# A hybrid attention block on one core: the keys' rotary step joins the plan, shuffles are given longer landing times, and filler products are placed otherwise

## The chip, the cores and the metric

The kernel runs on one core of one Trainium2 chip. The core has five engines that matter here, each with its own instruction queue that is worked off in order: TensorE (PE, matrix products and transposes), VectorE (DVE), ScalarE (ACT), GpSimd (POOL) and SyncE (SP), which here only starts DMA transfers. The metric is device time in microseconds of one execution; lower is better. The times before are the median of three runs.

## The reference

One encoder block, all in float32, for 512 real tokens of width 1024, ahead of which stand 16 learned meta tokens (528 columns in the kernel):

```python
u = rms_norm(h, pre_mix_gain[l])
proj = u @ w_in[l]
qa, ka, va, qb, kb, vb, g = jnp.split(proj, SPLITS, axis=-1)
qa = rope(qa...); ka = rope(ka...); qb = rope(qb...); kb = rope(kb...)
o_swa = windowed_gqa_sink_attention(qa, ka, va, attn_sink[l], pos, is_real)
o_diff = differential_attention(qb, kb, vb, lam, lambda_init, diff_subln_gain[l], is_key)
gates = jax.nn.sigmoid(g + b_gate[l]); g_swa, g_diff = gates[..., :D_MODEL], gates[..., D_MODEL:]
merged = g_swa * (o_swa @ w_branch_swa[l]) + g_diff * (o_diff @ w_branch_diff[l])
h = h + rms_norm(merged @ w_out[l], post_mix_gain[l])
u = rms_norm(h, pre_ffn_gain[l]); gate_up = u @ w_ffn_in[l]
f = (jax.nn.silu(gate_up[..., :D_FF]) * gate_up[..., D_FF:]) @ w_ffn_out[l]
h = h + rms_norm(f, post_ffn_gain[l])
```

The first branch (o_swa) is windowed attention with 16 query heads in four groups, each group with one key head, a band of three blocks of 128 keys, the meta keys and a sink. The second branch (o_diff) has 8 heads; each subtracts two softmaxes over all keys and is normalized over its own 128 channels. `rope` rotates the two halves of a head's 64 channels by angles that depend on the position.

## The kernel before

Every float32 matrix is split into a high part that TensorE takes exactly (`float32r`) and a low remainder; a product is then three matmuls (`mm3`, L283: high x high, high x low, low x high). A weight tile of 128 output channels is loaded by SyncE (512 KB), its high part is cast by ScalarE, and the remainder is subtracted by GpSimd or VectorE. There are three buffers each for the raw weights (`wr`), the high parts (`wh`) and the low parts (`wl`). A product of such a tile over 512 columns is 24 matmuls.

The work runs in these stages:

1. Start (to L505). The inputs are loaded and split, keys (`kA`, `kB`) and half of the values of the first branch are projected, and the factors of the first normalization are worked out. The rotation tables `rot` are multiplied by them. Then the keys' rotary step: `rope` (L466) takes the raw keys `kraw` in two halves of 264 columns, multiplies them by the tables on VectorE (L470, L471), adds on GpSimd (L472), and `split` writes high and low parts into a tile `hl`. Twelve DMA shuffles bring this to a layout that the score products can take, `KK[g]` for four groups: two from `hl` into the upper partitions of `KK[g]` (L488) and one that doubles these into the lower 64 partitions (L489). After these come loads of the lambda vectors and of two masks.
2. The plan (L508 to L979). `Plan` is a small planner that runs when the program is built. Every step is a `task` with an engine, a cost in us, the buffers that it reads, writes or keeps, and a priority. `Plan.run` walks through time: for each engine it takes the task that can start first, on TensorE by its priority alone, on the others by its ready time plus a slack from its priority. A task that writes a buffer follows all earlier writers and users of that buffer. Buffers stand in slots (`hl` 1, `kk` 4, `q` 8, `wr`, `wh`, `wl` 3, `ta` 2, `tb` 1, `S` 1). The result is the order of instructions on each engine; what really happens at run time is set by semaphores, and each engine follows its order. The planner's times are never used on the chip.
   In the plan are: the values of the first branch (`v_swa`), queries of four groups (`q_swa`, L650), the gates of the first branch (`gate`), the 16 units of windowed attention (`s_swa` scores and softmax, `t_swa` transposes and products with V), the heads of the second branch (`qk`, `vd`, `s_diff`, `t_diff`), the output projection of the first branch (`b1`, eight products) and the gates of the second (`gate2`, eight products). `rope_t` (L546) is the planned form of `rope`; `move` (L568) is the planned DMA shuffle, with 0.6 us of SyncE's time and a landing time `land` after it.
   On TensorE, attention steps have priorities 0, 1 and 8; the projections have 20 and a running number of the weight tile, and fill what the attention leaves ("fillers").
   The keys are not in the plan: the four `KK` tiles are given to it as held buffers that are ready at 9.0 us (L628 to L632). The tile `hl` is a single buffer, which the keys and each later group or head use in turn.
3. After the plan: the output projection of the second branch (L990), the sum, `w_out`, the second normalization, and the feed-forward layer (to L1175). Order and code of it are untouched.

At the start of the plan the engines' queues are joined with those of the start stage: within each of both the order is the program's, and the two are interleaved by the framework's scheduler.

Of the kernel before, what the change touches and what calls it, by code (L numbers as in the profile page):

```python
# [20 lines left out]
P = 128  # L21
# [215 lines left out]
def encoder(ctx, tc, I, out, dbg=None):  # L237
# [227 lines left out]

    def rope(hl, psa, psb, c0, n, o0, scale=None):  # L466

        ta = atp.tile([P, 2, HALF], F32, tag="ta", name="ta", bufs=2)[:, :, 0:n]
        tb = atp.tile([P, 2, HALF], F32, tag="tb", name="tb")[:, :, 0:n]
        dve.tensor_tensor(out=ta, in0=psa.unsqueeze(1).broadcast_to([P, 2, n]), in1=rot[:, 1:3, c0:c0 + n], op=ALU.mult)  # L470
        dve.tensor_tensor(out=tb, in0=psb.unsqueeze(1).broadcast_to([P, 2, n]), in1=rot[:, 0:2, c0:c0 + n], op=ALU.mult)  # L471
        pool.tensor_tensor(out=ta, in0=ta, in1=tb, op=ALU.add)  # L472
        split(hl[:, :, 0, o0:o0 + n], hl[:, :, 1, o0:o0 + n], ta, scale=scale)
        return ta

    def hl_tile():
        return zp.tile([P, 2, 2, KX], F32R, tag="hl", name="hl")

    hl = hl_tile()
    KK = [zp.tile([P, 2, KX], F32R, tag="kk", name="KK", bufs=4) for _ in range(4)]  # L480
    for s in range(2):
        cs = slice(s * HALF, (s + 1) * HALF)
        ta = rope(hl, kraw[0][:, cs], kraw[1][:, cs], s * HALF, HALF, s * HALF)
        if s == 0:
            split(hl[:, :, 0, EXT:KX], hl[:, :, 1, EXT:KX], ta[:, :, 0:NMETA])
    for g in range(4):
        for i in range(2):
            sp.dma_start(out=KK[g][32 * i:32 * i + 32].bitcast(F32), in_=hl[32 * g:32 * g + 32, i].bitcast(F32))  # L488
        sp.dma_start(out=KK[g][64:128].bitcast(F32), in_=KK[g][0:64].bitcast(F32))  # L489
# [56 lines left out]
    def rope_t(hl, pa, pb, c0, n, p0, o0, scale):  # L546
# [5 lines left out]
        def half(t, src, i):  # L552
# [3 lines left out]
        oh_, ol_ = (lambda: hl.t[:, :, 0, o0:o0 + n]), (lambda: hl.t[:, :, 1, o0:o0 + n])  # L556
# [5 lines left out]
        T("ACT", 0.18 + 0.55 * m, lambda: act.activation(out=oh_(), in_=ta.t[:, :, 0:n], func=AF.Copy, scale=scale),  # L562
          r=[ta], w=[hl], prio=3)
        T("DVE", 0.19 + 0.58 * m,
          lambda: dve.scalar_tensor_tensor(out=ol_(), in0=ta.t[:, :, 0:n], scalar=scale, in1=oh_().bitcast(F32),
                                           op0=ALU.mult, op1=ALU.subtract), r=[ta], w=[hl], prio=3, port=True)

    def move(out, in_, r, w, dep=(), land=1.6):  # L568
        return T("SP", 0.6, lambda: sp.dma_start(out=out().bitcast(F32), in_=in_().bitcast(F32)), r=r, w=w, dep=dep,  # L569
                 prio=2, land=land)  # L570
# [57 lines left out]
    KB = [pl.held("kk", KK[g]) for g in range(4)]  # L628
    MK = [pl.held("rt", t) for t in (mk1, mk2)]
    PV = [pl.held("tr", t) for t in pV]  # L630
    for b in KB:
        pl.ready(b, 9.0)  # L632
    for b in MK:
        pl.ready(b, 5.0)

# [30 lines left out]
    def s_swa(u):  # L666
# [11 lines left out]
        for hh in range(4):  # L678
# [3 lines left out]
            def prod(hh=hh, S=S):  # L682
                for x in range(2):
                    pe.matmul(out=Sw2[:, S.slot, 0:nk], lhsT=QS[g][hh].t[:, i * P:(i + 1) * P],  # L684
                              rhs=KK[g][:, x, r0:r1], start=(x == 0), stop=(x == 1))
            Ssteps[u].append(T("PE", 2 * mm_t(nk), prod, r=[QS[g][hh], KB[g]], w=[S], keep=[S0], prio=1))
# [16 lines left out]
    def t_swa(u):  # L703
# [5 lines left out]
        for n, (o, kb) in enumerate(blocks):  # L709
# [6 lines left out]
            Ttr[u].append(T("PE", 0.436, trans, r=ph, w=[tr], keep=[pt], prio=0, chain="tr"))  # L716
# [41 lines left out]
    def qk(h):  # L758
# [11 lines left out]
        for c in range(2):  # L770
            K = sb("kk", [P, 2, EXT], F32R, "Kd", 4, zp)
            Q = sb("q", [P, EXT], F32R, "Qd", 8)
            for i in range(2):
                move(lambda i=i, K=K: K.t[32 * i:32 * i + 32], lambda i=i, c=c: hl.t[64 + 32 * c:96 + 32 * c, i, :, 0:EXT],
                     [hl], [K], land=1.9)
            move(lambda K=K: K.t[64:128], lambda K=K: K.t[0:64], [], [K], land=2.2)
            for i in range(2):
                for x in range(2):
                    b = 2 * x + i
                    move(lambda b=b, Q=Q: Q.t[32 * b:32 * b + 32, 0:NTOK],  # L780
# [479 lines left out]
```

## Time and profile before

| what | value |
|---|---|
| median of 3 runs (lowest, highest) | 1012.42 us (1012.09, 1013.39) |
| profiled execution, its own time | 1011.81 us |
| its span, first to last instruction | 1010.0 us |
| mean granted TensorE clock | 0.988 of full speed |
| TensorE busy | 968.4 us, 96% |
| VectorE, ScalarE, GpSimd busy | 565.2, 450.6, 281.4 us |
| DMA moved | 109.33 MB |

The profile is of one execution. Its span is from the first to the last instruction, and the execution took 1.8 us more than that. An engine's "idle before" a row is the time in which it had nothing to run before that instruction, and the arrow names what it waited for last. The stages by time: start to about 25 us, first branch about 25 to 225, second branch about 225 to 551, the rest to the end.

### The profile page before, as it was taken

The numbers are of one execution on the slowest core, as the hardware profiler recorded it, in microseconds if no ns is written. First come the engines' busy times: TensorE is split into PE (matmuls) and PEld (weight loads), VectorE is DVE, ScalarE is ACT, GpSimd is POOL, SyncE is SP. The second block draws the span as 40 slices with busy tenths as digits, with TensorE's granted clock in tenths as the row PEclk, the third lists the DMA queues.
The fourth block names the chain that finished last, engine by engine and source line by source line (L and its number), as shares of the span: only waits on it lengthen the run. The fifth ranks groups of instructions, "written<-read, shape, count | busy, mean of one in ns | idle before, by whom it ended". The sixth has DMA issues, their size and how long they took to land.

```text
span 1010.0 us, 14259 instructions
## 1 busy us (share of the span) xinstructions
PE 968.4 (96%) x5355; PEld 833.9 (83%) x5355; DVE 565.2 (56%) x1015; ACT 450.6 (45%) x828; POOL 281.4 (28%) x242
## 2 busy tenths in 40 slices
PE   9879998999899999999799999999999999999997
PEld 9767888889698989998688888998888888888885
DVE  5736885888585647778664774853333333323224
ACT  6316773776455536366655343443223223222121
POOL 1343444533142232342221421464343310000000
PEclk9999999999999999999899999999999999999999
DMA  9463123241424342432623461252323333324222
GB/s 342 119 167 107 43 66 84 71 138 43 127 63 127 91 119 58 112 106 55 180 64 128 143 231 41 84 193 99 105 86 102 104 90 98 105 85 145 61 64 83
DMA packets 37140, 109.33 MB, mean 108 GB/s; under 512 B 6080, under 2 KB 6592, under 8 KB 37072
## 3 DMA queue, kind: packets, MB, share of 16 engines
q1 hardware_dynamic: 37072, 108.42, 35.4%
q8 instruction: 42, 0.69, 0.3%
q14 instruction: 26, 0.21, 0.1%
HBM read 87.04 MB, written 2.10 MB: 88 GB/s over the span
## 4 chain that ended last, share of the span: by engine, by line
PE 64%; DVE 3%; SPq 2%; DMA 1%; issue 1%; ACT 0%; DVEq 0%; ACTq 0%
PE pr L288 14%; PE pr L287 14%; PE pr L286 14%; PE Sd L818 3%; PE wk L288 2%; PE wk L287 2%; PE wk L286 2%; SPq L569 2%; PE tr L858 1%; PE acc L288 1%; PE tr L288 1%; PE acc L287 1%; PE tr L287 1%; PE acc L286 1%; PE tr L286 1%; PE Od L871 1%
## 5 line engine op out<-in xcount | busy, mean ns | idle before, releaser
L252 POOL TENSOR_TENSOR wl<-wr,wh 128x768 fp32r<-128x768 f32 (+1 forms) x76 | 168.0, 2212 | 244.7 <-ACT wh L271 159.4
L286 PE MATMUL pr<-xh,wh 128*128 128x264 f32 (+1 forms) x616 | 200.3, 325 | 0.0
L288 PE MATMUL pr<-xh,wl 128*128 128x264 f32 (+1 forms) x616 | 196.7, 319 | 2.2 <-DVE wl L252 2.2
L287 PE MATMUL pr<-xl,wh 128*128 128x264 f32 (+1 forms) x616 | 197.1, 320 | 0.2 <-DVE xl L378 0.2
L271 ACT CAST wh<-wr 128x1024 fp32r<-128x1024 f32 x78 | 82.1, 1052 | 232.1 <-PE pr L287 95.7
L252 DVE TENSOR_TENSOR wl<-wr,wh 128x1024 fp32r<-128x1024 f32 (+2 forms) x110 | 111.0, 1010 | 118.2 <-ACT wh L271 110.1
L288 PEld LDWEIGHTS pr<-xh,wl 128*128 128x128 f32 x616 | 116.4, 189 | 10.9 <-DVE wl L252 2.4
L287 PEld LDWEIGHTS pr<-xl,wh 128*128 128x128 f32 x616 | 116.7, 189 | 7.6 <-DVE xl L378 0.4
L286 PEld LDWEIGHTS pr<-xh,wh 128*128 128x128 f32 x616 | 116.7, 189 | 7.1
L287 PE MATMUL pr<-ul,wh 128*128 128x512 f32 (+1 forms) x304 | 110.7, 364 | 0.3 <-DVE ul L252 0.3
L286 PE MATMUL pr<-uh,wh 128*128 128x512 f32 (+1 forms) x304 | 110.9, 365 | 0.0
L288 PE MATMUL pr<-uh,wl 128*128 128x512 f32 (+1 forms) x304 | 110.6, 364 | 0.0
L528 ACT CAST wh<-wr 128x1024 fp32r<-128x1024 f32 x56 | 58.3, 1046 | 29.8 <-PE pr L287 19.6
L287 PEld LDWEIGHTS pr<-ul,wh 128*128 128x128 f32 x304 | 57.3, 189 | 9.6 <-DVE ul L252 0.5
L286 PEld LDWEIGHTS pr<-uh,wh 128*128 128x128 f32 x304 | 57.4, 189 | 9.2
L288 PEld LDWEIGHTS pr<-uh,wl 128*128 128x128 f32 x304 | 57.3, 189 | 9.0
L823 DVE TENSOR_REDUCE nm<-Sd 128x1 f32<-128x528 f32 x64 | 45.1, 705 | 34.0 <-PE Sd L818 33.3
L559 POOL TENSOR_TENSOR ta<-ta,tb 128x528 f32<-128x528 f32 (+1 forms) x24 | 34.7, 1446 | 76.2 <-DVE tb L553 56.2
L818 PE MATMUL Sd<-Kd,Qd 128*128 128x264 f32 x256 | 44.2, 295 | 11.0 <-DMA wr<-in_w_in_dram 5.3
L698 POOL TENSOR_SCALAR p<-p,rc 128x272 f32<-128x272 f32 (+1 forms) x64 | 37.6, 603 | 61.5 <-DVE rc L696 61.5
L308 POOL TENSOR_TENSOR r3y<-r3v,mhalf 128x1 f32<-128x1 f32 x4 | 2.2, 550 | 186.7 <-DVE r3v L307 186.7
L687 DVE CUSTOM_DVE_ANT_0 p<-Sw,mk,nsink 128x272 f32<-128x272 f32 (+1 forms) x64 | 34.6, 565 | 27.8 <-PE Sw L684 26.4
(369 smaller groups left out, 1993.8 us busy)
## 6 DMA issues: line engine op xcount, KB each, us to landing
wr<-in_w_in_dram SPq DMA_DIRECT2D x50, 512.0 KB, 3.7
wr<-in_w_fi_dram SPq DMA_DIRECT2D x50, 512.0 KB, 3.5
wr<-in_w_fo_dram SPq DMA_DIRECT2D x22, 512.0 KB, 3.5
Kd<-hl SPq DMA_DIRECT2D x32, 132.0 KB, 2.4
Kd<-Kd SPq DMA_DIRECT2D x16, 264.0 KB, 3.3
Q<-hl SPq DMA_DIRECT2D x64, 64.0 KB, 2.0
Qd<-hl SPq DMA_DIRECT2D x64, 64.0 KB, 2.5
wr<-in_w_bs_dram SPq DMA_DIRECT2D x8, 512.0 KB, 3.6
```

Of the source, the lines that this page charges most:

```text
L252: (eng or dve).tensor_tensor(out=lo, in0=src, in1=hi.bitcast(F32), op=ALU.subtract)
L271: act.copy(out=wh, in_=raw)
L286: pe.matmul(out=ps, lhsT=ah, rhs=bh, start=first, stop=False)
L287: pe.matmul(out=ps, lhsT=ah, rhs=bl, start=False, stop=False)
L288: pe.matmul(out=ps, lhsT=al, rhs=bh, start=False, stop=last)
L528: T("ACT", 1.05, lambda: act.copy(out=wh.t, in_=wr.t), r=[wr], w=[wh], prio=pr_)
L559: T("POOL", 0.05 + 1.3 * m, lambda: pool.tensor_tensor(out=ta.t[:, :, 0:n], in0=ta.t[:, :, 0:n], in1=tb.t[:, :, 0:n], op=ALU.add), r=[tb], ...
L569: return T("SP", 0.6, lambda: sp.dma_start(out=out().bitcast(F32), in_=in_().bitcast(F32)), r=r, w=w, dep=dep, prio=2, land=land)
L687: T("DVE", 0.21 + 0.5 * c, lambda hh=hh, S=S, h=h: dve.tensor_tensor_reduce(out=pt.t[:, hh, 0:nk], in0=Sw2[:, S.slot, 0:nk], in1=mask, sca ...
L698: T("POOL", 0.2 + 0.43 * c, lambda z=z: pool.tensor_scalar(out=pt.t[:, z, 0:nk], in0=pt.t[:, z, 0:nk], scalar1=rc.t[:, z:z + 1], scalar2=1 ...
L818: pe.matmul(out=S.t[:, s, 0:HALF], lhsT=Q[c].t[:, i * P:(i + 1) * P], rhs=K[c].t[:, x, s * HALF:(s + 1) * HALF], start=(x == 0), stop=(x = ...
L823: T("DVE", 0.71, lambda S=S, c=c, one=one: dve.tensor_reduce(out=nm.t[:, c, one], in_=S.t[:, :, 0:HALF], axis=AX.XY, op=ALU.min), r=[S], w ...
```

## The change

- The keys' rotary step and its 12 shuffles leave the start stage and become tasks of the plan. `rope` and `hl_tile` are gone; `rope_t` takes the raw keys and, by `more`, also writes the 16 meta columns a second time behind the others. The `hl` tile and the four `KK` tiles are now the plan's buffers. The loads of lambda and masks keep their place in the start stage, which now has no shuffles ahead of them.
- Landing times in the plan: shuffles 2.7 us instead of 1.6 (queries) and 1.9 (second branch's keys), the doubling of key tiles 4.0 instead of 2.2.
- Planned TensorE costs: score products get 0.08 us more in the first branch and 0.12 in the second; a group of four transposes 0.5 us instead of 0.436.
- Fillers: of the eight `b1` products, three, three and two stand with heads 0, 1 and 2, instead of two, three and three. `gate2` takes separate conditions for its weight loads (`early`) and its products (`dep`): tiles 4 to 7 now come first, their loads from the second and fourth score step of head 6 on and their products from the sixth; before, both came after the last score step of head 6. Tiles 0 to 3 come last, with loads after the last score step of head 6 and products after the last query shuffle of head 7; before, both after the first score step of head 7.

```diff
-    hl = hl_tile()
-    KK = [zp.tile([P, 2, KX], F32R, tag="kk", name="KK", bufs=4) for _ in range(4)]
-    for s in range(2):
-        cs = slice(s * HALF, (s + 1) * HALF)
-        ta = rope(hl, kraw[0][:, cs], kraw[1][:, cs], s * HALF, HALF, s * HALF)
-        if s == 0:
-            split(hl[:, :, 0, EXT:KX], hl[:, :, 1, EXT:KX], ta[:, :, 0:NMETA])
-    for g in range(4):
-        for i in range(2):
-            sp.dma_start(out=KK[g][32 * i:32 * i + 32].bitcast(F32), in_=hl[32 * g:32 * g + 32, i].bitcast(F32))
-        sp.dma_start(out=KK[g][64:128].bitcast(F32), in_=KK[g][0:64].bitcast(F32))
...
-    def rope_t(hl, pa, pb, c0, n, p0, o0, scale):
+    def rope_t(hl, pa, pb, c0, n, p0, o0, scale, more=False):
...
+        parts = [(o0, n, m)] + [(EXT, NMETA, 0.06)] * more
+        for o, w, f in parts:
+            T("ACT", 0.18 + 0.55 * f, lambda o=o, w=w: high(o, w), r=[ta], w=[hl], prio=3)
+        for o, w, f in parts:
+            T("DVE", 0.19 + 0.58 * f, lambda o=o, w=w: low(o, w), r=[ta], w=[hl], prio=3, port=True)
+
+    def move(out, in_, r, w, dep=(), land=2.7):
...
-    KB = [pl.held("kk", KK[g]) for g in range(4)]
-    for b in KB:
-        pl.ready(b, 9.0)
...
+    KB = []
+    KR = [buf(None, lambda t=t: t) for t in kraw]
+    hk = sb("hl", [P, 2, 2, KX], F32R, "hl", 1, zp)
+    for s in range(2):
+        rope_t(hk, KR[0], KR[1], s * HALF, HALF, s * HALF, s * HALF, 1.0, more=(s == 0))
+    for g in range(4):
+        K = sb("kk", [P, 2, KX], F32R, "KK", 4, zp)
+        for i in range(2):
+            move(lambda i=i, K=K: K.t[32 * i:32 * i + 32], lambda i=i, g=g: hk.t[32 * g:32 * g + 32, i], [hk], [K])
+        move(lambda K=K: K.t[64:128], lambda K=K: K.t[0:64], [], [K], land=4.0)
+        KB.append(K)
...
-            Ssteps[u].append(T("PE", 2 * mm_t(nk), prod, r=[QS[g][hh], KB[g]], w=[S], keep=[S0], prio=1))
+            Ssteps[u].append(T("PE", 0.08 + 2 * mm_t(nk), prod, r=[QS[g][hh], KB[g]], w=[S], keep=[S0], prio=1))
...
-            Ttr[u].append(T("PE", 0.436, trans, r=ph, w=[tr], keep=[pt], prio=0, chain="tr"))
+            Ttr[u].append(T("PE", 0.5, trans, r=ph, w=[tr], keep=[pt], prio=0, chain="tr"))
...
-                     [hl], [K], land=1.9)
-            move(lambda K=K: K.t[64:128], lambda K=K: K.t[0:64], [], [K], land=2.2)
+                     [hl], [K])
+            move(lambda K=K: K.t[64:128], lambda K=K: K.t[0:64], [], [K], land=4.0)
...
-                hd["S"].append(T("PE", 4 * mm_t(HALF), prod, r=[Q[c], K[c]], w=[S], prio=1))
+                hd["S"].append(T("PE", 0.12 + 4 * mm_t(HALF), prod, r=[Q[c], K[c]], w=[S], prio=1))
...
-            T("PE", 0.436, trans, r=A, w=[tr], keep=hd["keep"], prio=0, chain="tr")
+            T("PE", 0.5, trans, r=A, w=[tr], keep=hd["keep"], prio=0, chain="tr")
...
-    def gate2(js, tag, n, dep):
+    def gate2(js, tag, n, early, dep):
...
-            pg = products(weights(I["w_in"][44 + j], dep), X, X_, NMETA, EXT, dep)
+            pg = products(weights(I["w_in"][44 + j], early), X, X_, NMETA, EXT, dep)
...
-        for _ in range((2, 3, 3, 0, 0, 0, 0, 0)[h]):
+        for _ in range((3, 3, 2, 0, 0, 0, 0, 0)[h]):
...
-    gate2((0, 1, 2, 3), "hl", 1, heads[7]["S"][0:1])
-    gate2((4, 5), "kk", 4, heads[6]["S"][7:8])
-    gate2((6, 7), "kk", 4, heads[6]["S"][7:8])
+    S6 = heads[6]["S"]
+    gate2((4, 5), "kk", 4, S6[1:2], S6[5:6])
+    gate2((6, 7), "kk", 4, S6[3:4], S6[5:6])
+    gate2((0, 1, 2, 3), "hl", 1, S6[7:8], [heads[7]["moved"]])
```

26 lines of the change are left out of this document (7 added, 19 removed).

## The prediction

> **What bounds the kernel now.** I read the page's head first. Two numbers of it matter: the span and TensorE's busy time.
>
> ```profile
> span 1010.0 us, 14259 instructions
> PE 968.4 (96%) x5355; PEld 833.9 (83%) x5355; DVE 565.2 (56%) x1015; ACT 450.6 (45%) x828; POOL 281.4 (28%) x242
> ```
>
> TensorE sets the end, and the change neither adds nor removes a matmul. What it can move is the 1010.0 - 968.4 = 41.6 us in which TensorE stood still, and the time in which it ran at a lower granted clock. So the second view is the list of waits, TensorE's part (total us, times, longest):
>
> ```profile
> PE Sw L684 <- DMA Q<-hl: 7.7, 2, 6.1
> PE Sd L818 <- DMA wr<-in_w_in_dram: 5.3, 2, 3.2
> ...
> PE tr L587 <- DVE VT L581: 3.5, 2, 1.9
> ```
>
> The first two are score products (L684 first branch, L818 second) that waited for shuffled Q and K. The release named "wr" is a weight load that was issued among the last shuffles. The third view is TensorE's timeline, which gives each wait its place (start, length, work, then the idle time before it and its releaser):
>
> ```profile
> 37.12 0.28 PE L587 MATMUL tr<-ident,VT 128*16 128x128 f32 x1 [1.87 <-DVE VT L581]
> 74.74 0.60 PE L684 MATMUL Sw<-KK,Q 128*128 128x272 f32 x1 [6.13 <-DMA Q<-hl]
> 164.02 0.49 PE L684 MATMUL Sw<-KK,Q 128*128 128x272 f32 x2 [1.58 <-DMA Q<-hl]
> 271.33 0.82 PE L818 MATMUL Sd<-Kd,Qd 128*128 128x264 f32 x4 [3.18 <-DMA wr<-in_w_in_dram]
> 315.22 0.48 PE L818 MATMUL Sd<-Kd,Qd 128*128 128x264 f32 x2 [1.01 <-DMA Qd<-hl]
> 360.95 0.48 PE L818 MATMUL Sd<-Kd,Qd 128*128 128x264 f32 x2 [2.10 <-DMA wr<-in_w_in_dram]
> 406.72 0.48 PE L818 MATMUL Sd<-Kd,Qd 128*128 128x264 f32 x2 [1.24 <-issue]
> 483.20 0.55 PE L592 MATMUL tr<-ident,VT 128*128 128x128 f32 x3 [1.00 <-DVE VT L581]
> 485.26 0.55 PE L858 MATMUL tr<-ident,pa 128*128 128x128 f32 x3 [1.51 <-DVE Vdm L252]
> 490.33 1.22 PE L818 MATMUL Sd<-Kd,Qd 128*128 128x264 f32 x4 [2.73 <-DMA Qd<-hl]
> ```
>
> The fourth view is busy time in chosen stretches (the stretch, its length, then each engine's busy us; the granted TensorE clock comes behind POOL):
>
> ```profile
> 68.60:74.70 6.10, 0.00 (x1) 0.00 (x0) 2.44 (x2) 0.72 (x1) 3.56 (x2) 0.93 0.45 107
> 74.70:81.00 6.30, 6.26 (x19) 5.04 (x19) 2.02 (x10) 2.26 (x7) 0.97 (x2) 0.53 0.56 194
> 166.00:170.00 4.00, 3.77 (x15) 3.46 (x15) 1.37 (x8) 1.75 (x5) 0.96 (x2) 0.57 0.00 0
> 271.30:275.00 3.70, 3.67 (x12) 3.01 (x13) 1.47 (x3) 0.79 (x2) 0.71 (x1) 0.57 0.20 82
> 486.00:490.30 4.30, 1.60 (x6) 0.69 (x6) 2.06 (x4) 1.53 (x3) 0.00 (x0) 0.60 0.92 283
> 490.30:494.00 3.70, 3.67 (x14) 3.20 (x15) 2.42 (x3) 1.44 (x3) 2.38 (x1) 0.54 0.55 203
> ```
>
> After four of these waits TensorE works for some us at little over half clock. The loss is busy time times the missing share of the clock: 6.26 x 0.47 = 2.9 us after the first wait, 3.77 x 0.43 = 1.6 after the one at 164, 3.67 x 0.43 = 1.6 after 271, and 1.60 x 0.40 + 3.67 x 0.46 = 2.3 around 490. A wait removed gives its own length and this.
>
> **The keys' step, and the first wait (6.13 us).** Before, the keys' rotary work and their 12 shuffles stand ahead of the plan, which only assumes that the keys are there at 9.0 us (L632) and that the single hl buffer is free at once. SyncE's queue shows what happened:
>
> ```profile
> 41.19 1.23 SPq L488 DMA_DIRECT2D KK<-hl  x2
> ...
> 60.48 0.50 SPq L489 DMA_DIRECT2D KK<-KK  x1
> ...
> 65.15 10.33 SPq L569 DMA_DIRECT2D Q<-hl  x16
> ```
>
> Each doubling of a key tile (L489) waits in the in-order queue for its two halves to land, so 12 shuffles took 41.19 to 60.98, 19.8 us, and weight loads stood behind them. The queries of group 0 wait for hl:
>
> ```profile
> 60.51 0.63 ACT L562 ACTIVATE hl<-ta 128x512 fp32r<-128x512 f32 x1 [10.46 <-DMA KK<-hl]
> 50.02 1.29 POOL L559 TENSOR_TENSOR ta<-ta,tb 128x512 f32<-128x512 f32 x1 [9.42 <-DVE tb L553]
> KK<-hl SPq DMA_DIRECT2D x8, 136.0 KB, 3.7
> Q<-hl SPq DMA_DIRECT2D x64, 64.0 KB, 2.0
> ```
>
> The cast into hl could have started when POOL was done, 50.02 + 1.29 = 51.3, and started at 60.51. After the change the plan knows the keys' landings, and since it counts two writes of one tile as following each other, it issues the first halves of all four groups, then the second halves, then the doublings. The eight reads of hl then go out back to back: 41.19 + 8 x 0.62 (1.23 for two) + 3.7 to land = 49.9, under 51.3. So hl no longer holds the cast, which comes 9.2 us earlier, and with it the 16 shuffles, and the first scores at 74.74 - 9.2 = 65.5. TensorE is busy with fillers until 68.6: cover of 3.1 us. If that cover fails, the wait returns with the lateness beyond it. The loads of lambda and the masks, which came behind the keys at 61 to 65, now come ahead of them; no engine waits longer for it. **I take 6.13 + 2.9 = 9.0 us off; bounds 0 and 9.0.**
>
> The step's own instructions do not change in number: four DVE products, two POOL sums, three casts, three remainders, 12 shuffles. But by priority the plan sets keys' products ahead of V's scaling (L581) on DVE, three in 2 us. In the second V wait the opposite happened:
>
> ```profile
> 36.65 0.76 DVE L581 TENSOR_TENSOR VT<-pr,rbc 128x264 f32<-128x264 f32 x2
> ```
>
> V came late there because two products of the keys, unknown to the plan, stood ahead. Now the plan sees them and sets TensorE's w3 products ahead of the transposes. For the first V wait (3.5 - 1.9 = 1.6) DVE is 1.9 us later, and some five more w3 products of 0.36 cover 1.8, so nothing changes. **I take 1.0 off; bounds -1.9 (V later, uncovered) and +1.9.**
>
> **Longer landing times.** A query tile takes four shuffles, which the plan counts one behind the other: before 4 x (0.6 + 1.6) = 8.8 us, now 4 x (0.6 + 2.7) = 13.2. What they really take, in the last head:
>
> ```profile
> 477.48 0.64 SPq L569 DMA_DIRECT2D Kd<-hl  x1
> ...
> 488.07 0.51 SPq L569 DMA_DIRECT2D Qd<-hl  x1
> Kd<-Kd SPq DMA_DIRECT2D x16, 264.0 KB, 3.3
> ```
>
> From the first issue, 477.48, to the first score product, 490.33, it was 12.85 us. So the old figure was some 3 us short and the new one about right (the doubling: 4.0 against 3.3 measured). TensorE's order is fixed by the plan, so a score planned 3 us early is a wait with fillers standing behind it; planned later, the fillers go first. Every wait in the list of 164, 271, 315, 361 and 406 is of this kind and under 4.4 us, the amount by which the plan now holds the scores back. **I take all of them: 1.58 + 1.6, 3.18 + 1.6, and 1.01 + 2.10 + 1.24 = 4.35, together 12.3 us; bounds 0 and 12.3.** The small additions to matmul costs (0.08, 0.12, 0.436 to 0.5) work the same way; no price of their own.
>
> By the Trainium skill, page "TensorE: Matmul & The Clock Gate" (section "What's actually happening"), TensorE falls to half clock after an idle window of about 3.4 us. The stretches above disagree: 1.58, 3.18 and 2.73 us were followed by 0.57, 0.57 and 0.54 too, though 2.10 at 361 was not. By the page only the 6.13 us wait would give its clock back, and the sum below would be 1.6 + 1.6 + 2.3 = 5.5 us smaller.
>
> **The last gate products (gate2).** Four of the eight could start their loads only after the last score of head 6, at 481.33, four even later; in the wait for head 7's Q nothing was left to run.
>
> ```profile
> 474.37 0.66 PE L818 MATMUL Sd<-Kd,Qd 128*128 128x264 f32 x4
> ...
> 481.33 0.65 PE L818 MATMUL Sd<-Kd,Qd 128*128 128x264 f32 x4
> ...
> 528.59 0.40 PE L863 MATMUL Od<-aTm,Vdm 128*128 128x512 f32 x1
> ```
>
> These are the sixth and the last score of head 6 and the last transposed product of head 7. Now four gate products have loads from the second and fourth score of head 6 and products from the sixth: 4 x 5.4 us, against waits of 1.00 + 1.51 + 2.73. Their load issues (0.5 to 0.9 us each, three of them between the shuffles of 477 to 488) also leave the last shuffles. The price of a product and the end of this stage:
>
> ```profile
> 543.15 0.68 DVE L252 TENSOR_TENSOR dl<-ob,dh 128x512 fp32r<-128x512 f32 x1
> ...
> 551.03 0.69 DVE L935 TENSOR_TENSOR z<-pr,rbc 128x512 f32<-128x512 f32 x1 [4.27 <-PE pr L288]
> ...
> 561.92 0.69 DVE L994 SCALAR_TENSOR_TENSOR z<-z,pr 128x512 f32<-128x512 f32 x1 [1.44 <-PE pr L288]
> 567.36 0.69 DVE L994 SCALAR_TENSOR_TENSOR z<-z,pr 128x512 f32<-128x512 f32 x1 [1.44 <-PE pr L288]
> ```
>
> A product of 512 columns is 567.36 - 561.92 = 5.44 us. Used earlier, these fillers no longer cover head 7's normalization, which ends at 543.83. The next product (L993) needs that head in the last of eight steps, so 7/8 x 5.44 = 4.8 us after its start. It starts at 551.0 now and could start at 539.1: 11.9 us of slack, of which filling these waits takes 7.5. **I take 5.24 + 2.3 = 7.5 off; bounds 0 and 7.5.** The shift of one b1 product (2,3,3 to 3,3,2) only exchanges fillers; nothing.
>
> **What is given back.** Four unknowns, which the trace does not show. Fillers spent earlier lack between the last b1 and the sixth score of head 6:
>
> ```profile
> 372.61 0.69 DVE L924 SCALAR_TENSOR_TENSOR t<-t,pr 128x512 f32<-128x512 f32 x1
> ```
>
> There only head 4 starts late by 4.4 - 1.24 = 3.2 us, plus 1.6 of clock: 0 to 4.8, I take 2.5. The wait for head 7 ahead of L993: 0 (slack kept) to 15.2 - 4.8 = 10.4, where 15.2 is from its last transposed product at 528.59 to 543.83 with no filler left; I take 2.5, near the kept slack. Weight loads in the gaps that the longer landings leave between shuffles, 12 groups at up to 1.8 us (three loads of 0.6): 0 to 21.6, I take two exposed, 3.5. V and POOL order at the start: 0 to 1.9, I take 0.5. Together 9.0.
>
> **Sum:** 9.0 + 1.0 + 12.3 + 7.5 = 29.8, less 9.0, is 20.8 us off. The profiled execution took 1011.81 us for its span of 1010.0, and the median of the runs is 1012.42, 0.6 above. The span comes to 989.2, the median to 1012.4 - 20.8 = 991.6, rounded to 991.
>
> **Rivals.**
> 1. *The waits move rather than go.* The first stage is mended (9.0 + 1.0), but in heads 1 to 7 work is conserved and the held-back scores leave TensorE dry later, when only the Q, K and V products of the next heads are left. Against it: after each wait above fillers stood ready. For it: no filler is free between 372.61 and 474. Time: 1012.4 - 10 = 1002, with a part of the rest 999 to 1008.
> 2. *Slower: weight loads block the shuffles.* The plan now puts loads into the gaps between shuffles, and a load whose buffer is not yet free stops SyncE's whole queue, the rest of a head's shuffles with it.
>
> ```profile
> SPq L526 <- POOL wl L252: 92.2, 14, 15.8
> ```
>
> Such waits last 92.2 / 14 = 6.6 us on the mean. One in front of a head's last shuffles costs TensorE 6.6 + 1.6 of clock = 8.2. From four of the 12 groups on it eats the 29.8; with five it is 41 - 30 = 11 slower: 1023. Against it: none of these waits hit a group in the trace of before.
> 3. *It does not do what it says.* TensorE's order comes out as before wherever it waits, as the real landings and not the plan's set them: 1012.
>
> By the skill's rule of the clock gate, as weighed above, it would be 1012.4 - 15.3 = 997, in the forecast's own range.
>
> **How the numbers follow.** Forecast 0.65 (own range 979 to 999: all of the 29.8 and three more at one end, a gain of 13 at the other), rival 1 0.20, rival 2 0.10, rival 3 0.05. 0.2% (about 2 us) is what a measurement of this kernel can tell from no change. Faster: forecast and nearly all of rival 1, 0.84; same 0.05; slower 0.11. The range 979 to 1010 holds the forecast and rival 1 and leaves out rivals 2 and 3.
>
> **What would show it.** Right: hl's cast (now L562) no longer waits on KK<-hl; TensorE's wait for Q at the first L684 is under 1 us and the clock behind it stays at 1.0; the first scores of heads 1, 2, 3, 4 and 7 follow fillers without a gap; gate products stand between head 6's and head 7's scores. Wrong: a TensorE wait over 3 us ahead of L993 on dh or dl, or SyncE's weight loads with long waits among shuffles; or TensorE idle over 35 us in the whole span, which would mean that the waits only moved.

## The result, and the profile after

The changed kernel took 999.74 us (median of four runs, 996.66 to 1000.45), the kernel before 1012.9 us beside it (1012.09 to 1015.22). The ratio is 0.986 with a 95% interval of 0.9834 to 0.9887: faster by 11 to 17 us. The forecast was 991 us in a range of 979 to 1010. The sign and the range held; of the 20.8 us in the sum 13 to 14 came. Two executions in which the chip was far slower (1201 us with the keys' step alone, 5101 us with the split tiles below) are left out of all medians.

The head of the page of the changed kernel, profiled in an execution of 999.2 us:

```profile
span 997.3 us, 14285 instructions
PE 969.2 (97%) x5355; PEld 833.7 (84%) x5355; DVE 574.1 (58%) x1015; ACT 451.8 (45%) x828; POOL 278.7 (28%) x242
```

TensorE executed the same 5355 matmuls and stood still for 997.3 - 969.2 = 28.1 us instead of 41.6. These 13.5 us are about the gain of the span (12.7). What is left is seen in TensorE's part of the list of waits of the changed kernel (total us, times, longest):

```profile
PE Sw L674 <- DVE nm L677: 4.2, 9, 0.9
PE pr L286 <- ACT dh L898: 4.1, 1, 4.1
PE Sd L808 <- ACT pp L816: 3.1, 5, 1.0
PE Sw L674 <- issue: 2.1, 1, 2.1
```

(Line numbers have moved: the score products L684 and L818 are now L674 and L808, the shuffles L569 are L550, the keys' and queries' cast into hl is L536.) No wait for a shuffled Q or K of a second-branch head is left. Two waits of over 2 us remain: one at the first scores and a new one on dh, head 7's normalized output, in the tail. TensorE's timeline gives their places:

```profile
74.89 0.85 PE L674 MATMUL Sw<-KK,Q 128*128 128x272 f32 x4 [2.11 <-issue]
...
540.67 0.51 PE L286 MATMUL pr<-dh,wh 128*128 128x512 f32 x1 [4.12 <-ACT dh L898]
```

And busy time by stretch, of the kernel before and then of the changed one (the clock stands behind POOL's busy time):

```profile
110.00:250.00 140.00, 136.59 (x831) 118.13 (x830) 108.17 (x263) 94.11 (x223) 56.91 (x77) 0.99 0.27 76
250.00:420.00 170.00, 160.49 (x1070) 145.55 (x1070) 109.19 (x192) 84.66 (x157) 48.10 (x35) 0.99 0.35 96
480.00:540.00 60.00, 54.69 (x270) 44.08 (x269) 35.24 (x64) 37.25 (x66) 12.34 (x8) 0.94 0.38 111
```

```profile
110.00:250.00 140.00, 135.77 (x825) 116.90 (x824) 111.00 (x264) 95.20 (x221) 57.30 (x75) 0.99 0.27 77
250.00:420.00 170.00, 167.03 (x1135) 153.20 (x1135) 115.50 (x202) 86.19 (x161) 47.57 (x35) 1.00 0.40 109
480.00:540.00 60.00, 56.44 (x279) 45.91 (x277) 36.06 (x59) 35.44 (x60) 12.22 (x8) 1.00 0.28 86
540.00:560.00 20.00, 19.11 (x76) 15.50 (x77) 12.70 (x14) 5.85 (x8) 6.16 (x3) 0.91 0.30 88
```

In heads 1 to 4 (some 250 to 420 us) idle time fell from 9.5 to 3.0 us. From 480 to 540 us the clock is back at 1.00, but 3.6 us of idle time stand there still, and 0.9 us with a clock of 0.91 just behind: but for 0.3 us that is the wait on dh.

**The first scores.** The step that was forecast did begin as forecast. ScalarE, SyncE and POOL of the changed kernel:

```profile
52.04 0.63 ACT L536 ACTIVATE hl<-ta 128x512 fp32r<-128x512 f32 x1 [1.29 <-POOL ta L540]
```

```profile
49.28 3.72 SPq L550 DMA_DIRECT2D KK<-KK  x4
53.05 4.88 SPq L501 DMA_DIRECT2D wr<-in_w_in_dram  x3
57.97 8.71 SPq L550 DMA_DIRECT2D Q<-hl  x12
66.80 2.26 SPq L501 DMA_DIRECT2D wr<-in_w_in_dram  x2
69.11 2.41 SPq L550 DMA_DIRECT2D Q<-hl  x4
```

hl's cast waits for POOL only, at 52.04 instead of 60.51. But the first scores came at 74.89, where they had come at 74.74: SyncE issued five weight loads before and between the queries' shuffles, and the last four shuffles went out at 69.11 to 71.52. These four took 5.1 us to land (median); the 16 that went out together in the kernel before took 2.0.

**The tail.** The gate's last eviction came at 537.28 instead of 551.03, so TensorE reached head 7's output 13.75 us sooner. Head 7 itself came only 2.5 us sooner (its last step, the remainder dl, began at 540.65 instead of 543.15). ScalarE of the kernel before, then of the changed one, shows why:

```profile
535.00 1.28 ACT L985 ACT_TABLE_LOAD   x1
536.30 2.56 ACT L985 ACTIVATE z<-z,hb 128x512 f32<-128x512 f32 x4
538.77 0.61 ACT L896 ACTIVATE z<-y 128x512 f32<-128x512 f32 x1
```

```profile
529.04 0.63 ACT L885 ACTIVATE y<-y 128x512 f32<-128x512 f32 x1
529.69 1.28 ACT L976 ACT_TABLE_LOAD   x1
530.99 4.40 ACT L976 ACTIVATE z<-z,hb 128x512 f32<-128x512 f32 x7
535.29 0.62 ACT L886 ACTIVATE z<-y 128x512 f32<-128x512 f32 x1
...
540.00 0.62 ACT L898 CAST dh<-ob 128x512 fp32r<-128x512 f32 x1 [1.28 <-DVE ob L891]
```

Between two steps of head 7's normalization (L885 and L886) stand a table load and seven tanhs of the second gate, whose products now end early: 1.28 + 4.40 = 5.7 us in which TensorE's next operand waits in line. (L885 and L886 are L895 and L896 of the kernel before.) Four of the tanhs and the table load stood at this place already before the change; now it is seven.

### The profile page after: what moved, and what is told of

Its sections match the earlier page's. It is cut to its first block, busy times and chain, and to the rows that moved or that the text cites. A ratio compares the mean times of both kernels' runs of the same rounds, so it can differ in the third digit from the quotient of the medians.

```text
span 997.3 us, 14285 instructions
## 1 busy us (share of the span) xinstructions
PE 969.2 (97%) x5355; PEld 833.7 (84%) x5355; DVE 574.1 (58%) x1015; ACT 451.8 (45%) x828; POOL 278.7 (28%) x242
## 4 chain that ended last, share of the span: by engine, by line
PE 86%; DVE 7%; ACT 3%; issue 2%; SPq 1%; DMA 1%; DVEq 0%; ACTq 0%
PE pr L287 18%; PE pr L288 18%; PE pr L286 18%; PE Sd L808 3%; PE wk L288 2%; PE wk L286 2%; PE Sw L674 2%; PE wk L287 2%; PE tr L705 2%; PE O L717 2%; PE tr L288 2%; PE tr L287 2%; PE tr L286 2%; PE tr L848 2%; PE Od L861 1%
## 5 line engine op out<-in xcount | busy, mean ns | idle before, releaser
L816 ACT ACTIVATE pp<-Sd,nm 128x528 f32<-128x528 f32 x40 | 28.0, 700 | 46.4 <-DVE nm L813 27.7
L808 PE MATMUL Sd<-Kd,Qd 128*128 128x264 f32 x256 | 43.3, 291 | 3.3 <-ACT pp L816 3.1
```

The source lines that it names most:

```text
L808: pe.matmul(out=S.t[:, s, 0:HALF], lhsT=Q[c].t[:, i * P:(i + 1) * P], rhs=K[c].t[:, x, s * HALF:(s + 1) * HALF], start=(x == 0), stop=(x = ...
L816: T("ACT", 0.9, lambda S=S, c=c, one=one, p=p: act.activation(out=p().rearrange("p (a b) -> p a b", a=2), in_=S.t[:, :, 0:HALF], func=AF.E ...
```

## The experiments

Twelve kernels ran. The first theory: the change is the sum of three parts (keys in the plan, landing times, the gate's place), and what is missing of the forecast was lost in ScalarE's order in the tail and to the weight loads among the first shuffles. The rival: any edit makes the planner deal a new order, and no part has a price of its own.

### The tanhs behind head 7

```
-    behind(act.activation(out=z2[j], ..., func=AF.Tanh, ...), lnx[-1:])
+    behind(act.activation(out=z2[j], ..., func=AF.Tanh, ...), dhs[-1:])   # dhs: the casts to dh
```

> The changed kernel, in which the gates' tanhs (L976) are ordered behind head 7's cast to dh (L898) instead of behind the last normalization's start, so that seven tanhs and one table load no longer stand ahead of head 7's Square on ScalarE; TensorE's order is the same. Theory (the give-back sits in ScalarE's order at the tail): head 7's dh comes 5.7 us earlier (4.40 for the tanhs, 1.28 for the table load), the TensorE wait of 4.12 us at the first L286 on dh and its 1.6 us of slower clock go: 994 us against 999.7 for the changed kernel, ratio to the kernel before 0.981. Rival (the last products would wait for the gate's own STT, since the tanhs now come late): the wait moves to the last products or evictions and 1 us or less is gained: 998.5 to 1000.

It took 992.34 us, ratio 0.9815 (0.9797 to 0.9832). The order of TensorE, POOL and SyncE is the changed kernel's; around head 7's last steps only rows of ScalarE and two of VectorE stand otherwise, and elsewhere on these two engines a few neighbours change places. ScalarE, and the busy times of the tail:

```profile
526.84 0.63 ACT L885 ACTIVATE y<-y 128x512 f32<-128x512 f32 x1
527.50 0.63 ACT L886 ACTIVATE z<-y 128x512 f32<-128x512 f32 x1
...
531.00 0.62 ACT L898 CAST dh<-ob 128x512 fp32r<-128x512 f32 x1 [0.56 <-DVE ob L891]
531.64 1.28 ACT L976 ACT_TABLE_LOAD   x1
532.94 5.02 ACT L976 ACTIVATE z<-z,hb 128x512 f32<-128x512 f32 x8
```

```profile
480.00:540.00 60.00, 60.00 (x291) 49.30 (x292) 37.62 (x61) 36.79 (x62) 13.33 (x9) 1.00 0.28 88
540.00:560.00 20.00, 20.00 (x90) 16.56 (x89) 15.93 (x16) 7.24 (x9) 9.44 (x5) 1.00 0.48 157
```

From L885 to dh it is now 4.2 us instead of 11.0, and TensorE is busy without a gap from 480 to 560 us at full clock. The theory's 994 us was met and passed; the rival's wait at the last products did not come. The medians differ by 7.4 us, the ratios by 4.6 us of 1012.9, and the trace accounts for 4.12 us of wait and 19.11 x 0.09 = 1.7 us of clock, 5.8 in all; this execution also lost 2.9 us less to the clock ahead of the edit (last section). This is the version that beats both kernels.

### One part undone at a time

```
keys out:    rope(...) and the 12 shuffles ahead of the plan again; KB = held; ready at 9.0
old landing: move(..., land=1.6); heads: land=1.9 and land=2.2
old gate:    gate2((0,1,2,3), ...) first, behind heads[7]["S"][0:1]; (4,5), (6,7) behind heads[6]["S"][7:8]
```

> The changed kernel with the keys' rotary work and shuffles back outside the plan, as before; landing times, fillers' places and costs as changed. Theory (the parts add up, each worth what the landmarks show): the first branch loses its lead of 5.7 us (second branch's first scores at 225 instead of 219.4), the rest stays: 1005.5 us, and hl's cast waits for the keys' shuffles again until about 60 us. Rival (any edit deals a new order, and the lead is not the keys'): anything from 996 to 1010, the first scores not later than 75.5 us.

> The changed kernel with the old landing times (1.6 us for a shuffle, 1.9 and 2.2 us in the heads); the keys' own doubled shuffle keeps 4.0 us. Theory (the landing times took the waits at the heads' first scores away): waits of 3 us or more on the shuffled Q or K return at two to four of the heads' starts and the second branch gives back 5 to 12 us: 1005 to 1010 us. Rival (the other parts moved the fillers so that the starts are covered anyway): no wait of over 2 us at a head's start, 998 to 1001 us.

> The changed kernel with the second gate's fillers in the old order and under the old conditions (the four of one tag first, from head 7's first scores on, the others from head 6's last). TensorE's order differs only from about 440 us on. Theory (the gate's place is worth what the tail gained): the wait at head 7's first scores is back (5 us before) and the gate's last products end after head 7's dh, so that the wait of 4.12 us on dh is gone: 1003 to 1005 us. Rival (the wait at head 7's start had gone by the landing times already): 996 to 999 us, as the tail's wait on dh goes and nothing comes back.

| undone | us (median) | ratio to before | interval |
|---|---|---|---|
| nothing (the changed kernel) | 999.74 | 0.986 | 0.9834 to 0.9887 |
| keys' step | 1005.52 | 0.9936 | 0.9918 to 0.9955 |
| landing times | 1005.14 | 0.9939 | 0.9924 to 0.9954 |
| gate's place | 1001.61 | 0.990 | 0.9879 to 0.9922 |

With the keys out, hl's cast waits for the keys' shuffles again (ScalarE), and the wait at the first scores is back and longer than before the change (TensorE):

```profile
61.61 0.63 ACT L560 ACTIVATE hl<-ta 128x512 fp32r<-128x512 f32 x1 [11.89 <-DMA KK<-hl]
```

```profile
81.94 0.79 PE L690 MATMUL Sw<-KK,Q 128*128 128x272 f32 x2 [8.88 <-DMA Q<-hl]
```

That it is longer than before is the new landing times' doing; "Weight loads and the first shuffles" below shows how.

With the old landing times a head waits for its queries again, which no head did in the changed kernel:

```profile
405.39 0.73 PE L808 MATMUL Sd<-Kd,Qd 128*128 128x264 f32 x4 [3.68 <-DMA Qd<-hl]
```

Of the two to four head starts that the theory wanted with 3 us or more, this is the only one; a wait of 1.82 us at head 1's start and one of 3.16 us at the first scores came besides it. Both this kernel and the one with the keys out came to the time that was expected (1005 to 1010 and 1005.5). By the ratios, which carry 2 to 3 us of uncertainty each, undoing the keys' step costs 7.7 us, the landing times 8.0 and the gate's place 4.1; by the medians it is 5.8, 5.4 and 1.9.

With the gate's old place there is no wait on dh. But the wait at head 7's first scores did not come back as a wait for shuffles either: the longer landing times had dealt with that. What came is waits on the softmax of the heads there:

```profile
470.86 0.76 PE L808 MATMUL Sd<-Kd,Qd 128*128 128x264 f32 x4 [1.84 <-ACT pp L816]
...
475.59 0.47 PE L848 MATMUL tr<-ident,pp 128*128 128x128 f32 x1 [3.19 <-DVE pp L829]
```

So at 1001.61 both expectations for the gate were missed, the theory's 1003 to 1005 by 1.4 us and the rival's 996 to 999 by 2.6.

### One part alone

The same three parts, each put into the kernel before.

> The kernel before with the keys' rotary work and shuffles in the plan (with landing times of 2.7 and 4.0 us for these twelve shuffles alone); all else as before. Theory (the keys' part alone gives the lead of the first branch and no more): second branch's first scores 4 to 6 us earlier than 225.1, and 1006.5 to 1009 us in all. By the sum on record the part was worth 9.0 us: 1004. Rival (weight loads and queries' shuffles share SP's queue in the plan's order, so the first scores come no earlier and nothing is gained): 1011 to 1014 us.

> The kernel before with the longer landing times alone (2.7 us, 4.0 us for the doubled keys of the heads). Theory: the waits at 271, 315, 361 and 406 us go and the second branch is 5 to 10 us shorter: 1003 to 1008 us. By the sum on record 12.3 us less what is given back for late head starts: about 1002.5. Rival (the plan deals other waits): within 3 us of 1012.5.

> The kernel before with the second gate's fillers placed as changed, all else as before. TensorE's order differs only from about 450 us on. Theory: the wait at head 7's first scores (5.24 us and 2.3 us of clock) goes, and a wait for head 7's dh of about 4 us and 1.6 us of clock comes: 1010 to 1012 us, a gain of 1 to 2 us where the sum on record had 7.5 less 2.5. Rival (the tanhs do not stand ahead of head 7's Square in this order): no wait on dh, 1005 us.

| alone | us (median) | ratio to before | interval | gain in us (ratio x 1012.7) | in the sum on record |
|---|---|---|---|---|---|
| keys' step | 1007.07 | 0.9953 | 0.9931 to 0.9974 | 4.8 | 9.0 + 1.0 |
| landing times | 1005.17 | 0.992 | 0.9895 to 0.9945 | 8.1 | 12.3 |
| gate's place | 1010.35 | 0.998 | 0.9965 to 0.9995 | 2.0 | 7.5 |

All three times were as the theory had them; in the details the second branch began 3.8 us earlier with the keys' step (4 to 6 expected), and the wait on dh was half of what was expected. Within their uncertainty of 1.5 to 2.7 us each the parts add up: 4.8 + 8.1 + 2.0 = 14.9 us against 14.2 for all of them (0.014 x 1012.9). And each is smaller than its term.

With the keys alone the first scores came without a wait (at 73.60 us), but an earlier one took its place, in V's transposes:

```profile
40.60 0.90 PE L574 MATMUL tr<-ident,VT 128*128 128x128 f32 x3 [4.29 <-DVE VT L563]
```

VectorE and POOL of the same run show what made V late:

```profile
35.77 4.43 DVE L533 SCALAR_TENSOR_TENSOR hl<-ta,hl 128x528 fp32r<-128x528 f32 x2
40.12 0.42 DVE L563 TENSOR_TENSOR VT<-pr,rbc 128x264 f32<-128x264 f32 x1
```

```profile
35.02 2.37 POOL L252 TENSOR_TENSOR wl<-wr,wh 128x1024 fp32r<-128x1024 f32 x1 [0.28 <-ACT wh L504]
...
37.60 2.56 POOL L252 TENSOR_TENSOR wl<-wr,wh 128x1024 fp32r<-128x1024 f32 x1 [0.21 <-ACT wh L504]
```

Two remainders of the keys, one of 528 elements and a short one of 32 for the meta columns, took 4.43 us while POOL split two weight tiles, and V's scaling stood behind them. A remainder of 528 took 0.71 us in the same run (at 41.08) with nothing beside it. In the changed kernel, where POOL's second split began only at 38.28, the same pair took 2.29 us and V's wait was 1.1 us. From 38.2 to 45.0 us the granted clock was 0.50; before the change such a stretch (0.51 from 73.8 to 80.7) lay behind the 6.13 us wait.

The 16 query shuffles went out together in this run, but only from 62.43 us on, 2.7 us earlier than before the change: three weight loads stood ahead of them in SyncE's queue from 53.37 to 62.38.

With the landing times alone the softmax waits in the heads grew from 0.8 us in all to 7.7. TensorE's part of its list of waits:

```profile
PE Sd L818 <- ACT pp L826: 7.7, 7, 2.0
```

With the gate's place alone, a wait on dh appears here too:

```profile
552.66 0.50 PE L286 MATMUL pr<-dh,wh 128*128 128x512 f32 x1 [2.19 <-ACT dh L908]
```

### The gate's place and the tanhs

The last kernel with one more edit, the same as in the first experiment.

> The kernel before with the second gate's fillers placed as changed (that alone was 1010.4 us) and with the gate's tanhs behind head 7's dh; TensorE's order is the same as with the first edit alone. Theory (the gate's place is worth what was forecast less the new waits on the softmax of 3.3 us, and ScalarE's tanhs ate the rest): the wait of 2.2 us on dh and 1.6 us of clock go: 1006 to 1007 us. Rival (head 7's dh is late for other reasons): 1009.5 to 1011 us.

It took 1005.79 us, ratio 0.993 (0.991 to 0.995) instead of 0.998: 5.1 us by the ratios, with TensorE's order the same. The rival's 1009.5 to 1011 is out, and the theory's 1006 was just passed. The trace accounts for 2.19 us of wait and 1.7 us of clock, 3.9 in all; the rest is within the uncertainty. The gate's place together with the right order on ScalarE is worth 7.1 us (5 to 9), alone 2.0. That 7.1 lies so near the 7.5 of the sum is in part chance, as waits of 1.48 and 1.86 us on the softmax, ahead of head 6's scores, came with the new place and stand in both runs.

### Weight loads and the first shuffles

The plan counts four writes into one query tile one behind the other. Here each of the four gets a part of its own, with the tanhs placed late as well:

```
+    QP[g] = [[buf() for _ in range(4)] for _ in range(4)]
-    move(..., [hl], [QS[g][hh]])
+    move(..., [hl], [QP[g][hh][b]], keep=[QS[g][hh]])
-    T("PE", ..., prod, r=[QS[g][hh], KB[g]], w=[S], ...)
+    T("PE", ..., prod, r=[QS[g][hh], KB[g]] + QP[g][hh], w=[S], dep=[pc], ...)   # pc: the unit's sink copy
```

> The changed kernel with the tanhs behind head 7's dh (that alone was 992.3 us), and with the four shuffles of a first-branch query tile kept by the plan in four parts, so that it no longer counts them one behind the other; SyncE then issues the 16 shuffles of a group without weight loads between them. Theory (the loads among the shuffles held the first scores back): the 16 shuffles of the first group take about 10 us from 58, the first scores come at about 70 instead of 74.8 as far as TensorE's fillers leave it free, its wait of 1.9 us there goes: 989 to 991 us. Rival (loads held back behind 16 shuffles starve the products instead, or the new order costs elsewhere what it gives here): 993 to 998 us.

The theory's mechanism was seen, and so was the rival's, but the time lies outside both ranges. SyncE and TensorE of this run:

```profile
53.33 8.46 SPq L501 DMA_DIRECT2D wr<-in_w_in_dram  x3
61.84 10.38 SPq L550 DMA_DIRECT2D Q<-hl  x16
```

```profile
68.14 0.77 PE L675 MATMUL Sw<-KK,Q 128*128 128x272 f32 x4
```

The shuffles go out as one group, and although they begin 3.9 us later than in the changed kernel, the first scores come at 68.14, 6.75 us earlier, without a wait. The interleaved order was what held them back.

This edit takes away two things at once, and the other runs separate them: the plan dealt the shuffles to the four tiles in turn, and it put weight loads between them. A round of four shuffles takes SyncE 4 x 0.6 = 2.4 us of the plan's time. With 1.6 us to land, the next write of the same tile may follow after 2.2 us, so the rounds follow each other without a gap; with 2.7 us it may follow after 3.3, and the plan fills the gap. In all five kernels with the old landing time for queries (the one before, and those with the old landing times, the keys' step alone, the gate's place alone, and the gate with the tanhs) the 16 shuffles go out together, and the first scores come 9.6 to 11.2 us after the first shuffle is issued. In all kernels with the new one and whole tiles, two weight loads stand in front of the last four shuffles, and it is 14.3 to 16.9 us. With the split tiles it is 6.3. So, by these differences, dealing in turn holds the first scores by some 3 us, and the loads by another 5 to 7. With the landing times alone the first scores come at 79.16, 4.4 us later than before the change, behind a wait of 5.03 us.

The time was nevertheless 1000.2 us, ratio 0.9876 (0.9854 to 0.9899), 6 us slower than with the late tanhs alone. TensorE's part of its list of waits:

```profile
PE Sd L809 <- ACT pp L817: 6.1, 3, 3.0
PE tr L573 <- DVE VT L562: 5.5, 2, 4.3
```

The same 4.3 us wait for V as with the keys alone, and 6.1 us of waits on the softmax in the heads, where the order came out otherwise. At the start of the second branch the kernel is ahead (its first scores come at 214.05 instead of 216.67 with the late tanhs alone), and behind it gives back more than that.

### Small numbers of the plan

```
nudge:     move(..., land=2.8)          (2.7 in the changed kernel)
b1 split:  (2, 3, 3, 0, ...)            (3, 3, 2 in the changed kernel; tanhs late)
old costs: 2 * mm_t(nk), 4 * mm_t(HALF), 0.436   (0.08 + ..., 0.12 + ..., 0.5; tanhs late)
```

> The changed kernel with a landing time of 2.8 us instead of 2.7 us in the plan, so 4 per cent of one of its numbers. It measures how far the plan's order answers to a small nudge. Theory (the terms are robust): 998 to 1001.5 us, the starts of the heads without waits of over 2 us. Rival (the order is dealt anew by each edit, and single edits can't be priced to better than that): 3 us or more away from 999.7 us in either direction.

> The changed kernel with the tanhs behind head 7's dh (992.3 us alone), and with the b1 fillers split 2, 3, 3 over heads 0 to 2 as before the change, instead of 3, 3, 2. Theory (only an exchange of fillers, as on record): 991 to 994 us. Rival (one more filler in head 2 covers a later start, one fewer in head 0 uncovers one): 2 us or more away on either side.

> The changed kernel with the tanhs behind head 7's dh (992.3 us alone), and with the old matmul costs in the plan (no 0.08 and 0.12 us on the score products, 0.436 instead of 0.5 us for the transposes). Theory (no price of their own, as on record): 990.5 to 994 us. Rival (the additions spread the score products, and without them the waits on the softmax, 7.5 us in all at L674 and L808, grow): 995 to 999 us.

The nudge: 1001.05 us, ratio 0.9871 (0.9843 to 0.9899), beside 0.986. The total is robust, as the theory had it, but not the places: the wait at the first scores is gone, the 4.3 us wait for V is there, and the wait on dh is 2.2 us. The b1 split: 996.2 us, 0.9833 (0.9806 to 0.986). The old costs: 996.1 us, 0.9832 (0.9812 to 0.9853). Both lie 1.7 us above the 0.9815 of the late tanhs by their ratios, and 2 us outside the 994 that was expected, so by their medians both fall into their rivals' ranges. That rival's reason for the old costs is not borne out: its waits on the softmax at L674 and L808 were 7.9 us in all, against 7.5 with the late tanhs alone; what came is the 4.3 us wait for V. The intervals overlap, so whether these two parts are worth anything stays open. Neither is worth more than about 5 us.

## Why the prediction was right, and where it was not

The order of size, the sign and the range held, and three of the four named marks of a right forecast were seen: hl's cast no longer waits on KK<-hl, heads 1, 2, 3, 4 and 7 begin without a wait for a shuffle, gate products stand between head 6 and head 7. The fourth, a wait under 1 us at the first scores with the clock at 1.0 behind it, was not: it was 2.11 us, and the clock 0.79. Of the marks of a wrong forecast, the wait on dh over 3 us came (4.12), and in part the weight loads among shuffles, at the first group. TensorE's idle time, 28.1 us, stayed under the 35 that would have meant that the waits only moved. In number the time lies closer to the first rival's 1002 than to 991; it is 0.7 us outside the forecast's own range of 979 to 999 and inside that rival's 999 to 1008, so only the wider range, which covers both, held. It is not that rival's mechanism as a whole: in the changed kernel most of the waits in the heads did not move, they went (9.5 to 3.0 us from 250 to 420 us). (The forecast's own 991.6 rounds to 992.)

**The keys' step: 9.0 + 1.0 forecast, 4.8 measured alone.** The step that failed is that the cast "comes 9.2 us earlier, and with it the 16 shuffles, and the first scores at 74.74 - 9.2 = 65.5". The shuffles did not come with the cast. With the keys' step alone, three weight loads stood ahead of them and they began 2.7 us earlier; the wait at the first scores went, but the V wait grew from 1.87 to 4.29 us, with the clock loss behind it. That leaves 6.13 - (4.29 - 1.87) = 3.7 us, and the second branch began 3.8 us earlier. In the changed kernel the cast came 8.5 us earlier and the shuffles began at 57.97, 7.2 us earlier, but the first scores came 16.9 us after that instead of 9.6, as the landing times put weight loads among the shuffles. The prediction knew this rule of the plan (it counts the four writes of a query tile one behind the other, and lists loads in the gaps as a give-back of 3.5 us for all groups), but in the keys' step it kept the 16 shuffles as long as they were before the change. In this one group the loads alone hold the first scores by 7.3 us.

**The V wait.** I took 1.0 off and bounded the loss by 1.9. In the changed kernel the two V waits are 1.8 and 1.1 us, 2.9 in place of 3.5, so 0.6 went; but with four other orders (the keys alone, the nudge, the split tiles, the old costs) the second was 4.3 us. The bound failed because it counted only the order on VectorE, and not that an instruction there can take a multiple of its time beside POOL (4.43 us for a long and a short remainder, where a long one took 0.71 with nothing beside it). The rows above show the two side by side; no run moves POOL's split alone.

**Landing times: 12.3 forecast, 8.1 alone.** The mechanism was right: the waits at 271, 315, 361 and 406 us are gone in the changed kernel, and a wait of 3.68 us returns at a head's start with the old numbers. Mis-sized are two things. With the landing times alone TensorE stood still for 33.9 us instead of 41.6, so 7.7 us of waits went, though waits on the softmax in the heads grew to 7.7 us and the first scores came later; and of the 3.2 us of clock in the term nothing is seen, as the mean clock of that execution was 0.987, and 0.988 before. In the changed kernel it is the wait at 164 us: the one for Q went, and waits on the softmax there took its place (L674 on nm, up to 0.9 us each), so that stretch gained nothing: from 110 to 250 us TensorE was idle for 140 - 136.59 = 3.4 us before and 4.2 after, both at a mean clock of 0.99. The forecast's 2.5 us for a late head 4 was too much: the longest wait of the kind that such a head would show, L808 on pp, is 1.0 us.

**The gate's place: 7.5 forecast, 2.0 alone, 7.1 with the tanhs late.** The fillers did cover head 7's start. What failed is the give-back "The wait for head 7 ahead of L993: 0 (slack kept) to 15.2 - 4.8 = 10.4", of which 2.5 was taken as "near the kept slack". The slack was worked out with head 7's end fixed relative to its last product (15.2 us), as if that chain were only its own. It is not: the gate's tanhs share ScalarE with it, and when the gate is early, they come due in the middle of the normalization. The trace of before already showed it: four tanhs and the table load stood in that chain (535.00 to 538.77). The wait was 4.12 us and cost 1.7 us of clock besides, 5.8 instead of 2.5, and one edit to ScalarE's order takes all of it away.

**The sum.** With the terms as measured alone, 4.8 + 8.1 + 2.0 = 14.9, and 14.2 measured together; the forecast's terms were 29.8 less 9.0 of give-back. Three of the four give-backs named the right places (loads among shuffles, V at the start, head 7's wait) with the wrong weights, and the three large terms above them had been taken at their upper bounds. The rival by which any edit deals a new order is right about the places of the waits and wrong about the total for the one small nudge (1 to 2 us), but the split tiles show that it can decide: first scores 6.75 us earlier ended 6 us slower.

## What to carry to other kernels

When filler work is moved earlier, follow what it feeds, not only what it covers: its evictions and activations come due earlier too, and in an in-order engine they may land in the middle of the chain that the fillers used to hide. When a planner's rule is used to predict one part of an order, apply it to every part that has the same shape. And take a planner's gain at its upper bound only where the next wait behind the removed one is known: here the waits at the first scores, at 164 us and ahead of head 7 each had a second one near them, on V, on the softmax or on head 7's output.

## What was unexpected of the hardware

**The clock behind a short wait is not a function of the wait.** The changed kernel and the one with the late tanhs give TensorE the same order, and up to 170 us nearly the same waits. The stretches of the first and then of the second:

```profile
74.00:82.00 8.00, 6.12 (x22) 4.62 (x23) 3.12 (x13) 3.75 (x12) 2.10 (x3) 0.79 0.22 68
150.00:170.00 20.00, 17.85 (x96) 14.86 (x95) 12.14 (x32) 10.34 (x24) 9.87 (x12) 0.91 0.25 73
```

```profile
74.00:82.00 8.00, 5.88 (x26) 4.03 (x26) 3.76 (x16) 4.26 (x13) 2.51 (x3) 1.00 0.20 71
150.00:170.00 20.00, 17.85 (x110) 15.08 (x108) 14.03 (x37) 12.67 (x31) 9.88 (x12) 1.00 0.27 80
```

A wait of 2.11 us was followed by a lower clock and one of 1.90 us at the same place was not; 17.85 us of work in 20 went once at 0.91 and once at 1.00. These two differences are 6.12 x 0.21 + 17.85 x 0.09 = 2.9 us, and the second branch began 2.75 us earlier in the second execution. Each drop is half the clock for 3.4 us (a granted 0.51 from 77.0 to 80.5 and from 162.3 to 165.8 us), so it costs 1.7 us where TensorE has work; the traces of the other kernels show drops of 3.4, 6.8 and 10.2 us. The changed kernel's own four runs spread over 3.8 us. The kernel before, run 20 times beside the single parts, spread from 1009.92 us to 1016.53 with mean clocks of 0.989 to 0.981, and its longest execution had the lowest clock. So the forecast's clock terms of 1.6 us each were prices of one execution and not of the kernel. The Trainium skill (page "TensorE: Matmul & The Clock Gate", section "What's actually happening") says that the window in which activity is judged runs freely and does not start with the kernel; that agrees with these rows. Its idle window of about 3.4 us does not: no single wait in these stretches was that long, and the clock still fell in one execution of the two.

**VectorE beside POOL.** In the changed kernel a cast of 16x256 took 2.50 us beside a split of weights on POOL. VectorE's rows, then POOL's:

```profile
34.49 0.28 DVE L594 CAST Vm<-Vm 16x256 fp32r<-16x256 f32 x1
...
38.33 2.50 DVE L594 CAST Vm<-Vm 16x256 fp32r<-16x256 f32 x1
```

```profile
38.28 2.40 POOL L252 TENSOR_TENSOR wl<-wr,wh 128x1024 fp32r<-128x1024 f32 x1 [1.19 <-ACT wh L503]
```

The first of the two casts had begun ahead of such a split and took 0.28 us. The long one ends where POOL's instruction ends (38.28 + 2.40 = 40.68), within 0.15 us. The Trainium skill (page "SBUF — State Buffer", section "Who interferes with whom") describes an exclusive lock on a port pair that the two engines share, held for a whole instruction; the times agree with waiting for the other's end, and not with a shared rate.
